# Twelve of fourteen pairs of column tiles by seven block products, and an order by matmul count for every engine

## The chip, the cores and the metric

The kernel runs on one core of one Trainium2 chip. The time is the device time of one execution in microseconds (us); the profile adds one execution recorded by the hardware profiler.

## What is computed

One residual block on 1024 tokens of 1024 channels, all in float32. The input is normalised per token, one projection gives eight parts of 512 columns, two mixers use them, and an output projection, a residual and a last norm follow.

```python
h = rmsnorm(x, norm_gain)                              # [1024, 1024]
q, f_logit, i_in, z_a, u, gate_b, gate_c, z_b = split(h @ w_in)   # 8 x 512 columns
f = lb + (1 - lb) * sigmoid(f_logit)                   # 4 heads of 128
o_a = hgrn2_chunkwise(q, log f, 1 - f, i_in)           # chunks of 64 tokens, state 128x128
o_a = rmsnorm_per_head(o_a) * hgrn_norm_gain * silu(z_a)
y_b = gate_b * causal_conv3(gate_c * u)
o_b = rmsnorm_per_64_channels(y_b) * conv_norm_gain * silu(z_b)
x = x + concat(o_a, o_b) @ w_out
out = rmsnorm(x) * final_norm_gain
```

## The kernel before, in words

**Products.** Every operand of a large product is split into two float32r parts, high and low (`split_part`, L96 to 98: ScalarE copies the high part, VectorE subtracts it for the low one). A product of one 128x128 block with 512 columns is then three matmuls (high x high, high x low, low x high), here called *main* products: `pe.mm` at L44 issues each of them. x lies transposed in `XH` and `XL`, channels on partitions, without its norm's factor; that factor (`rst` per token, `R` spread over partitions) is multiplied in when a result is read from PSUM.

**Stages.** First unit v (L156 to 173): the values `i_in` with tokens on partitions, contraction outermost, all eight PSUM banks at once, 192 main products, while x and the weights come in. Then come column tiles of 128 channels on partitions, each two halves of 512 tokens, `project` (L226): 24 main products a half. For each of four heads f and q (`head`, L239), then for each of four conv tiles u, c, b, z (`conv`, L339). Then z_a with tokens on partitions (192) and the output projection (384, the last tile in two halves of 256 columns). That is 24 column tiles of 48; in all 1896 main products of 512 columns and 48 of 256.

**The recurrence.** For each head, `forget` values give cumulated decays `e` (scan, L257) and their reciprocals (L260), and from them `kh` and `qh`. Eight steps follow, one per pair of chunks: `scores` (L287: a product and a transpose on PE, a copy on ACT, a masked copy into `sc` on DVE, L296) and `combine` (L298: up to three products, L306 to L309; the new state on DVE, L317). These small products are put between the main products of the next tiles: `Stream.later` (L49) files a step with the number of main products after which it is due, and `mm` (L43) issues one due step after each main product; `STEP` (13) main products lie between two combines.

**Norm sums of the conv group.** `norm` (L361): the squares of y, split, are multiplied by a 128x128 matrix `bones` of 1/64, which sums 64 partitions and spreads the sum at once: two products of 512 columns for each half tile (L364, L365), then square root, reciprocal and scale (L366 to L369).

**What sets the order.** PE and SP (the queue that issues the DMAs) run in program order; VectorE, ScalarE and GpSimd are ordered by the scheduler, with a priority for the states (L314). PSUM: `psa`, four banks for column tiles, `psb`, four for small steps. Weights go through three staging buffers and six buffers each of high and low parts.

Of the kernel before, what the change touches and what calls it, by code (L numbers as in the profile page):

```python
# [16 lines left out]
P = 128  # L17
# [8 lines left out]
WB = 6       # weight units on chip  # L26
STEP = 13    # main matmuls between the steps of a head's recurrence
NLAG = 44    # main matmuls between a conv tile and its norm's sums
NWARM = 8
AHEAD = 200  # priority of the recurrence's state over other elementwise work  # L30
TLAG = 22    # main matmuls between a gate's product and its transposes

# columns of the packed per-partition constants
C_NG, C_HLB, C_CW, C_CG = 0, 8, 16, 28
NCOL = 32

class Stream:
# [14 lines left out]

    def flush(self):
        while self.heap:
            heapq.heappop(self.heap)[2]()

@with_exitstack
def hybrid_block(ctx: ExitStack, tc: tile.TileContext, xT, x, wtok, wcol, wout, cols, hgain, fgain, out):
# [16 lines left out]

# [8 lines left out]
    ga = const.tile([P, W], F32, name="ga")  # L84

# [1 line left out]
    units = [("v", kp, wtok[0, kp]) for kp in range(4)]  # L87
    for h in range(NH):
        units += [("f", h, wcol[2 * h + 1]), ("q", h, wcol[2 * h])]
    for j in range(4):  # L90
        units += [(c, j, wcol[8 + 4 * j + i]) for i, c in enumerate("ucbz")]
    units += [("za", kp, wtok[1, kp]) for kp in range(4)]
    units += [(f"o{n}", kp, wout[n, kp]) for n in range(2) for kp in (2, 3, 0, 1)]
    split, issued = {}, [0]

    def split_part(hi, lo, raw):  # L96
        A.copy(hi, raw)
        V.tensor_tensor(lo, raw, hi.bitcast(F32), op=ALU.subtract)  # L98
# [12 lines left out]
    def need(c, i):
        pos = next(p_ for p_, u in enumerate(units) if u[0] == c and u[1] == i)
        fetch(pos + WB)
        return split[c, i]

# [1 line left out]
    pv = [(psa if t < 4 else psb).tile([P, W], F32, tag="ps", name=f"pv{t}") for t in range(NT)]  # L117

    def split_x(k, raw, t0, t1):
        g = col[:, C_NG + k:C_NG + k + 1]  # L120
        rv = raw.rearrange("p (t c) -> p t c", c=P)[:, t0:t1]
        A.activation(XH[:, t0:t1, k, :], rv, AF.Copy, scale=g)
        V.scalar_tensor_tensor(XL[:, t0:t1, k, :], rv, g, XH[:, t0:t1, k, :].bitcast(F32), op0=ALU.mult,
                               op1=ALU.subtract)

    rstart = const.tile([P, W], F32, name="rstart")
    V.memset(rstart[:, :P], 0.0)
    V.memset(rstart[:, P:], 0.0)
    for _ in range(NWARM):  # warms TensorE up while the first loads run
        T.matmul(pv[NT - 1][:, :P], rstart[:, :P], rstart[:, :P], start=True, stop=True)  # L130
# [8 lines left out]
    for t in range(0, NT, 2):  # L139
        nc.sync.dma_start(raw[:, t * P:(t + 2) * P], xT[0, :, t * P:(t + 2) * P])  # L140
        if t == 0:
            nc.sync.dma_start(col, cols)
# [191 lines left out]
    for h in range(NH):  # L334
        head(h)
# [232 lines left out]
```

## Time and profile before

| quantity | value |
|---|---|
| median of 3 runs | 502.87 us (502.83 to 503.73) |
| span of the profiled execution, first to last instruction | 500.7 us |
| what lies around the span, by the median | 2.2 us |
| busy: PE, DVE, ACT, POOL | 491.8, 257.6, 172.7, 157.4 us |
| granted TensorE clock, mean over the span | 0.997 of full speed |
| moved by DMA | 38.93 MB |

The busy time of an engine is what the profile counts inside its instructions; a share of it says nothing yet of a stage, so the views by stretch and the timelines come after it. No time of the profiled execution as a run is listed beside its span; the median of the runs is taken for it. The page's chain of work that ended last holds only the last steps on VectorE and is not used here.

### The profile page before, as it was taken

The numbers are of one execution on the slowest core, as the hardware profiler recorded it, in microseconds if no ns is written. First come the engines' busy times: TensorE is split into PE (matmuls) and PEld (weight loads), VectorE is DVE, ScalarE is ACT, GpSimd is POOL, SyncE is SP. The second block draws the span as 40 slices with busy tenths as digits, with TensorE's granted clock in tenths as the row PEclk, the third lists the DMA queues.
The fourth block names the chain that finished last, engine by engine and source line by source line (L and its number), as shares of the span: only waits on it lengthen the run. The fifth ranks groups of instructions, "written<-read, shape, count | busy, mean of one in ns | idle before, by whom it ended". The sixth has DMA issues, their size and how long they took to land. (4 is left out here: it accounts for less than half of the span.)

```text
span 500.7 us, 5886 instructions
## 1 busy us (share of the span) xinstructions
PE 491.8 (98%) x2288; PEld 402.9 (80%) x2288; DVE 257.6 (51%) x363; ACT 172.7 (34%) x301; POOL 157.4 (31%) x143
## 2 busy tenths in 40 slices
PE   9999999999999999999999999999999999999995
PEld 7778887888888888888888888888888888888884
DVE  4342688948668335285647266552933461132323
ACT  5557722233223223170243127122722341123322
POOL 1000044524315003353658975233432122211000
PEclk9999999999999999999999999999999999999998
DMA  7778621110011110202111111112030171001342
GB/s 218 245 255 258 220 87 43 42 43 13 31 43 43 43 43 8 65 13 85 43 43 42 43 42 42 47 47 76 8 119 0 42 232 42 2 0 63 126 159 93
DMA packets 12699, 38.93 MB, mean 78 GB/s; under 512 B 1536, under 2 KB 2048, under 8 KB 12672
## 3 DMA queue, kind: packets, MB, share of 16 engines
q1 hardware_dynamic: 12672, 38.56, 23.2%
q8 instruction: 18, 0.29, 0.3%
q14 instruction: 9, 0.07, 0.0%
HBM read 34.36 MB, written 4.19 MB: 77 GB/s over the span
## 5 line engine op out<-in xcount | busy, mean ns | idle before, releaser
L44 PE MATMUL po<-wh_o,XL 128*128 128x512 f32 (+1 forms) x136 | 52.0, 382 | 0.0
L44 PE MATMUL po<-wl_o,XH 128*128 128x512 f32 (+1 forms) x136 | 52.0, 382 | 0.0
L44 PE MATMUL po<-wh_o,XH 128*128 128x512 f32 (+1 forms) x136 | 51.9, 382 | 0.0
L253 POOL TENSOR_SCALAR k<-f 128x512 f32<-128x512 f32 x8 | 5.0, 621 | 88.2 <-DVE f L251 88.2
L44 PEld LDWEIGHTS po<-wl_o,XH 128*128 128x128 f32 x136 | 25.5, 188 | 5.5
L44 PEld LDWEIGHTS po<-wh_o,XH 128*128 128x128 f32 x136 | 25.5, 188 | 5.4
L44 PEld LDWEIGHTS po<-wh_o,XL 128*128 128x128 f32 x136 | 25.5, 188 | 5.4
L368 DVE RECIPROCAL rs<-rs 128x512 f32<-128x512 f32 x8 | 26.8, 3353 | 3.7 <-ACT rs L367 3.5
L260 DVE RECIPROCAL ei<-e 128x128 f32<-128x128 f32 x32 | 27.1, 909 | 0.3
L44 PE MATMUL pp_f<-XH,wl_f 128*128 128x512 f32 x64 | 26.3, 411 | 0.0
L44 PE MATMUL pv<-wl_v,XH 128*128 128x512 f32 x64 | 25.6, 400 | 0.6 <-DVE wl_v L98 0.5
L44 PE MATMUL pp_q<-XH,wh_q 128*128 128x512 f32 x64 | 26.0, 407 | 0.0
L44 PE MATMUL pp_f<-XL,wh_f 128*128 128x512 f32 x64 | 26.0, 406 | 0.0
L44 PE MATMUL pp_q<-XH,wl_q 128*128 128x512 f32 x64 | 25.8, 403 | 0.0
L44 PE MATMUL pp_q<-XL,wh_q 128*128 128x512 f32 x64 | 25.8, 403 | 0.0
L44 PE MATMUL pp_f<-XH,wh_f 128*128 128x512 f32 x64 | 25.8, 403 | 0.0
L44 PE MATMUL pza<-wl_za,XH 128*128 128x512 f32 x64 | 25.7, 402 | 0.0
L354 POOL TENSOR_TENSOR cu<-us,R 128x512 f32<-128x512 f32 x8 | 11.3, 1418 | 45.9 <-DVE us L353 45.7
L44 PE MATMUL pv<-wh_v,XH 128*128 128x512 f32 x64 | 25.7, 401 | 0.0
L44 PE MATMUL pp_u<-XH,wl_u 128*128 128x512 f32 x64 | 25.6, 400 | 0.0
L44 PE MATMUL pp_c<-XH,wh_c 128*128 128x512 f32 x64 | 25.5, 399 | 0.0
L44 PE MATMUL pp_u<-XL,wh_u 128*128 128x512 f32 x64 | 25.5, 399 | 0.0
(181 smaller groups left out, 1261.1 us busy)
## 6 DMA issues: line engine op xcount, KB each, us to landing
xr<-x SPq DMA_DIRECT2D x8, 512.0 KB, 4.4
raw_o<-wout SPq DMA_DIRECT2D x8, 512.0 KB, 3.2
xo<-x SPq DMA_DIRECT2D x16, 256.0 KB, 3.4
rawx<-xT SPq DMA_DIRECT2D x7, 512.0 KB, 4.1
out<-y SPq DMA_DIRECT2D x7, 512.0 KB, 2.8
raw_f<-wcol SPq DMA_DIRECT2D x4, 512.0 KB, 3.7
raw_q<-wcol SPq DMA_DIRECT2D x4, 512.0 KB, 5.1
raw_u<-wcol SPq DMA_DIRECT2D x4, 512.0 KB, 3.2
```

The lines of the kernel that those rows point to most:

```text
L44: self.T.matmul(*args, **kw)
L253: G.tensor_scalar(kk, f, -1.0, 1.0, op0=ALU.mult, op1=ALU.add)
L260: V.reciprocal(ei[:, c0:c0 + W // 4], e[:, c0:c0 + W // 4])
L354: G.tensor_tensor(cu[:, 2 + o0:2 + o0 + W], us[hf], rs, op=ALU.mult)
L368: V.reciprocal(rs2, rs2)
```

## The change

**Pairs.** The 24 column tiles of f, q, u, c, b, z and the four of z_a (now also with channels on partitions) are taken in 14 pairs: u with c, f with q, b with z for each of h = 0 to 3, and two pairs of z_a. A pair is a 2x2 block product: the weight blocks B11, B12, B21, B22 (512 channels x 128 columns each) by the blocks A11, A12, A21, A22 of x (512 tokens x 512 channels). The first `NPLAIN` = 2 pairs take eight block products (P1 to P8), the other twelve take seven (M1 to M7), on the differences S1 to S4 of x blocks and T1 to T4 of weight blocks. A block product is 12 main products.

**Where the differences are made.** S1 to S4 are built in place over x by VectorE (`x_sum`) and split under the plain pairs, by the table `work` (key: block of 12 main products since the start of v's second half). T1 to T4 go to the two PSUM banks of `pst` (`t_sum`) and are split from there; `prepare` starts that `LEAD` = 5 block products ahead. x now carries its norm's factor, so `R` goes (`normalise`); the first half of v runs on x without it. Partial results that two outputs share are copied out of PSUM by ScalarE (`keep`) and added by VectorE (`add`).

**Order of all engines.** All five orders are written by hand. `Stream.at` files work for any engine at a number of main products, and `due` issues it; small PE steps come at least `SPACE` = 5 main products apart, combines `STEP` = 18 apart. `psa` has four banks, `psb` two.

**Norm sums.** Squares stay float32 and are not split; they are the stationary operand, and a 128x2 `bones` the moving one, four 2-column products for each half tile; a transpose, a store to memory and two loads spread the factor over partitions again. The reciprocal square roots outside the last norm are powers of -0.5 on GpSimd (`rsqrt`).

**Start.** v is done in two halves of 512 tokens; weights and x come in pieces of 128x512.

Three places of the order. On TensorE, at the norm sums of the first conv tile, before (`pp_z` is the PSUM tile of z, `sh` and `sl` the split squares):

```order
L44 MATMUL pp_z0_0_1801<-XH_81,wl_z0_1203 128x512
L44 MATMUL pp_z0_0_1801<-XH_81,wh_z0_1202 128x512
L44 MATMUL pp_z0_0_1801<-XL_82,wh_z0_1202 128x512
L364 MATMUL pss0_0_1822<-sh0_0_1759,bones_412 128x512
L365 MATMUL pss0_0_1822<-sl0_0_1761,bones_412 128x512
L44 MATMUL pp_z0_0_1801<-XH_81,wl_z0_1203 128x512
```

and now (`pb` and `pd` are banks of pair 3, `hB11` and `lT1` parts of its weight operands, `b0_0` the squares):

```order
L60 MATMUL pb_3_1094<-XH_89,hB11_3_965 128x512
L60 MATMUL pb_3_1094<-XL_90,hB11_3_965 128x512
L60 MATMUL pb_3_1094<-XH_89,lB11_3_966 128x512
L600 MATMUL pss0_0_1129<-bones_125,b0_0_983 128x2 x4
L60 MATMUL pd_3_1137<-XH_89,hT1_3_991 128x512
L60 MATMUL pd_3_1137<-XL_90,hT1_3_991 128x512
L60 MATMUL pd_3_1137<-XH_89,lT1_3_992 128x512
```

The two products of 512 columns became four of 2 columns (x4), and they stand between two block products of a later pair.

On VectorE, at the decays of head 0, before (`f` and `e` are its gate and decays, the scan stands as SCALAR_TENSOR_TENSOR at L257, `wl_` are low parts of weights, `qh` the query times decay):

```order
L251 TENSOR_SCALAR f0_1_568<-fl0_1_565,oml_435,lb_433 128x512
L282 TENSOR_TENSOR qh0_0_621<-pp_q0_0_596,er0_0_534 128x512
L254 COPY rstart_97<-f0_1_568 128x8
L255 MEMSET f0_1_568 128x8
L257 SCALAR_TENSOR_TENSOR e0_1_574<-f0_1_568,rstart_97 128x512
L260 RECIPROCAL ei0_1_576<-e0_1_574 128x128 x4
L264 COPY gt0_479<-e0_1_574 128x8
L98 TENSOR_TENSOR wl_q3_653<-raw_q3_651,wh_q3_652 128x1024
L296 COPY_PREDICATED sc0_414<-mask_405,psc0_0_660 128x128
L277 TENSOR_TENSOR gg0_588<-gt0_479 128x7
L296 COPY_PREDICATED sc1_415<-mask_405,psc0_1_672 128x128
```

and now (`z0` and `b0` are the sums of pair 2, `lT`, `lB` low parts of pair 3, `mb` the conv result):

```order
L463 TENSOR_TENSOR qh0_0_797<-qh0_0_797,e0_0_946 128x512
L314 TENSOR_TENSOR lT2_3_1041<-T2_3_1034,hT2_3_1040 128x512
L430 SCALAR_TENSOR_TENSOR e0_1_1070<-kh0_1_758,zeros_97 128x64 x3
L314 TENSOR_TENSOR lB22_3_1067<-B22_3_937,hB22_3_1066 128x512
L430 SCALAR_TENSOR_TENSOR e0_1_1070<-kh0_1_758,zeros_97 128x64 x5
L397 TENSOR_TENSOR z0_1_1089<-pb_2_897,m5_2_956 128x512
L397 TENSOR_TENSOR b0_1_1092<-pb_2_897,m4_2_1061 128x512
L305 TENSOR_TENSOR T4_3_1095<-B21_3_863,T2_3_1034 128x512
L446 RECIPROCAL ei0_1_1098<-e0_1_1070 128x128
L635 TENSOR_TENSOR mb_93<-mb_93,b0_1_1092 128x512
L446 RECIPROCAL ei0_1_1098<-e0_1_1070 128x128
L314 TENSOR_TENSOR lT4_3_1103<-T4_3_1095,hT4_3_1102 128x512
L479 COPY_PREDICATED sc0_129<-mask_122,psc0_0_1111 128x128
```

The one scan of 512 columns became eight of 64, the reciprocals stand apart, and between them and ahead of the first mask (`sc0`) stand the differences, low parts and sums of the pairs.

On SP, the loads at the start, before:

```order
L138 DMA raw_v0_109<-wtok 128x512
L140 DMA rawx0_108<-xT 128x256
L142 DMA col_87<-cols 128x32
L140 DMA rawx0_108<-xT 128x256 x3
L143 DMA raw_v0_109<-wtok 128x512
L159 DMA rawx1_156<-xT 128x1024
L153 DMA xr0_160<-x 128x1024
L159 DMA rawx2_187<-xT 128x1024
L106 DMA raw_v1_189<-wtok 128x1024
L153 DMA xr1_197<-x 128x1024
```

and now:

```order
L164 DMA wv0_135<-wv 128x512
L176 DMA x0_0_139<-xT 128x512
L178 DMA col_94<-cols 128x36
L164 DMA wv1_156<-wv 128x512
L176 DMA x0_1_160<-xT 128x512
L164 DMA wv2_176<-wv 128x512
L176 DMA x0_2_180<-xT 128x512
L188 DMA vo_92<-x 128x1024
L164 DMA wv3_198<-wv 128x512
L176 DMA x0_3_202<-xT 128x512
L188 DMA vo_92<-x 128x1024
```

Halves of x and of the weights alternate in 256 KB pieces, where whole rows of x (512 KB) and pairs of weight rows were loaded before.

The core of the diff:

```diff
+STEP = 18
+SPACE = 5
+LEAD = 5
...
+OPERAND = {"M1": (A11, "B11"), "M2": (A12, "B21"), "M3": (S4, "B22"), "M4": (A22, "T4"), "M5": (S1, "T1"),
+           "M6": (S2, "T2"), "M7": (S3, "T3")}
+ORDER = ["M1", "M5", "M2", "M6", "M3", "M4", "M7"]
...
+PLAIN = ["P5", "P6", "P7", "P8", "P1", "P2", "P3", "P4"]
+OPERAND.update({"P1": (A11, "B11"), "P2": (A12, "B21"), "P3": (A11, "B12"), "P4": (A12, "B22"), "P5": (S3, "B11"),
+                "P6": (S4, "B21"), "P7": (S3, "B12"), "P8": (S4, "B22")})
...
-        if self.heap and self.heap[0][0] <= self.n:
...
+        self.due()
+        if self.heap and self.heap[0][0] <= self.n and self.n >= self.last + SPACE:
+            self.last = self.n
             heapq.heappop(self.heap)[2]()
+            self.due()
...
+    def due(self):
+        while self.work and self.work[0][0] <= self.n:
+            heapq.heappop(self.work)[2]()
...
+    psa = ctx.enter_context(tc.tile_pool(name="psa", bufs=1, space=PSUM))
+    psb = ctx.enter_context(tc.tile_pool(name="psb", bufs=2, space=PSUM))
+    pst = ctx.enter_context(tc.tile_pool(name="pst", bufs=2, space=PSUM))
...
+    def rsqrt(ap):
+        G.tensor_tensor(ap, ap, mhalf[:, :ap.shape[1]], op=ALU.pow)
...
+    SUMS = {S3: ((0, 0), (0, 0), (1, 0), ALU.subtract), S1: ((1, 0), (1, 0), (1, 4), ALU.add),
+            S2: ((1, 4), (1, 4), (0, 0), ALU.subtract), S4: ((0, 4), (0, 4), (1, 4), ALU.subtract)}
+    def x_sum(which, k, eng):
+        (h0, k0), (h1, k1), (h2, k2), op = SUMS[which]
+        eng.tensor_tensor(x_at(h0, k + k0), x_at(h1, k + k1), x_at(h2, k + k2), op=op)
...
+    bones = const.tile([P, 2], F32, name="bones")
+    G.memset(bones, 0.0)
+    G.memset(bones[0:64, 0:1], 1.0 / 64)
+    G.memset(bones[64:128, 1:2], 1.0 / 64)
...
+    for k in range(NK):
+        load_wv(k)
+        load_x(0, k)
+        if 2 <= k < 6:
+            row_sum(k - 2)
+        if k == 6:
+            stats(0)
+        if k == NK - 1:
+            load_x(1, V_ORDER[1][0])
+            load_x(1, V_ORDER[1][1])
+            half_row_sum(0)
+            half_row_sum(1)
...
+    def t_sum(n, name):
+        b = raws[n]
+        x, y = {"T1": ("B12", "B11"), "T2": ("B22", "T1"), "T3": ("B22", "B12"), "T4": ("B21", "T2")}[name]
+        sums[n, name] = pst.tile([P, W], F32, tag="t", name=f"{name}_{n}")
+        V.tensor_tensor(sums[n, name], b[x], b[y] if y in b else sums[n, y], op=ALU.subtract)
...
+    def split_w(g):
+        n, step = products[g]
+        name = OPERAND[step][1]
+        src = raws[n][name] if name in raws[n] else sums[n, name]
+        hi = hip.tile([P, W], F32R, tag="hi", name=f"h{name}_{n}")
+        lo = lop.tile([P, W], F32R, tag="lo", name=f"l{name}_{n}")
+        A.copy(hi, src)
+        pe.at(4, lambda: V.tensor_tensor(lo, src, f32(hi), op=ALU.subtract))
+        ops[n, name] = hi, lo
...
+    def prepare(g):
...
+        if name[0] == "T" and (n, name) not in sums:
+            if name == "T4" and (n, "T2") not in sums:
+                t_sum(n, "T2")
+            t_sum(n, name)
...
+        pe.at(3, lambda: split_w(g))
...
+        prepare(g + LEAD)
+        product(ps, OPERAND[step][0], ops.pop((n, OPERAND[step][1])), first, resumed=not first)
+        if step in ("M1", "M4", "M5", "M6"):
+            keep({"M1": "m1", "M4": "m4", "M5": "m5", "M6": "u2"}[step], n, ps)
+        elif step == "M2":
+            c11(ps, kept.pop((n, "m1")))
+        elif step == "M3":
+            c12(ps, kept.pop((n, "u2")))
+        else:
+            c22(ps, kept.pop((n, "m5")))
+            c21(ps, kept.pop((n, "m4")))
+    def add(out_, ps, t):
...
+                for i in range(8):
+                    pe.at(i, lambda i=i: scan(i * CH))
...
+                pe.at(9, inverse)
+                for i in range(4):
+                    pe.at(9 + 5 * i, lambda c0=i * P: V.reciprocal(eis[0][:, c0:c0 + P], e[:, c0:c0 + P]))
+                pe.at(27, lambda: G.tensor_tensor(kh, kh, eis[0], op=ALU.mult),
+                      lambda: G.tensor_tensor(ev[:, :, 0, :], ev[:, :, 0, :],
+                                              eis[1][:, :, 0, CH - 1:CH].to_broadcast([P, 4, CH]), op=ALU.mult),
...
+            pe.at(2, lambda: A.copy(kts[pr], psc[:, 1]),
+                  lambda: V.copy_predicated(scbuf[(h * NT + pr) % NS], mask.bitcast(I32), psc[:, 0]))
...
-        def norm(hf, sh, sl):
-            pss = psb.tile([P, W], F32, tag="ps", name=f"pss{j}_{hf}")
-            T.matmul(pss, bones, sh, start=True, stop=False)
-            T.matmul(pss, bones, sl, start=False, stop=True)
...
+        def norm(hf, sq):
+            nm = f"{j}_{hf}"
+            pss = psb.tile([P, 2, 4], F32, tag="ps", name=f"pss{nm}")
+            for t in range(4):
+                T.matmul(pss[:, :, t], sq[:, t * P:(t + 1) * P], bones, start=True, stop=True)
+            r2 = sm.tile([P, 2, 4], F32, tag="r2", name=f"r2{nm}")
+            pe.at(3, lambda: A.activation(r2, pss, AF.Identity, bias=epsc, scale=1.0))
+            pe.at(10, lambda: rsqrt(r2.rearrange("p g t -> p (g t)")))
...
+            def to_rows():
+                prr = psb.tile([2 * 4, P], F32, tag="ps", name=f"prr{nm}")
...
+                rr = sm.tile([2 * 4, P], F32, tag="rr", name=f"rr{nm}", bufs=1)
...
+                pe.at(9, lambda: store(rr))
...
+            def store(rr):
+                rows = dram.tile([2 * 4, P], F32, tag="rows", name=f"rows{nm}")
+                nc.sync.dma_start(rows, rr)
+                pe.at(22, lambda: load(rows))
...
+                for g in range(2):
+                    nc.sync.dma_start(rs2[g * 64:(g + 1) * 64, :],
+                                      rows[g * 4:(g + 1) * 4].rearrange("t p -> (t p)").partition_broadcast(64))
+                pe.at(28, lambda: scale(rs2))
...
+        0: O(0, 0, 1) + N(0, 0) + [L(6)] + O(0, 2) + N(0, 1) + O(0, 3) + H(2, 3) + N(0, 2),
+        1: [L(7)] + N(0, 3, 4) + H(4, 5) + N(0, 5) + B(A11, 0),
+        2: [L(0), lambda: fetch(0, *first)] + H(6, 7) + N(0, 6, 7) + B(A11, 1),
+        3: [L(1)] + B(A11, 2, 3) + [lambda: stats(1)] + B(A12, 0),
+        4: [L(2)] + SW(0) + B(A12, 1, 2),
+        5: [L(3)] + SW(1) + B(A12, 3),
+        6: N(1, 0, 4) + SW(2),
+        7: N(1, 1, 5) + SW(3),
+        8: O(1, 0, 1) + N(1, 2, 6) + [lambda: fetch(1, *first)] + O(1, 2, 3),
+        9: N(1, 3, 7),
+        10: X(S3, 0, 1),
+        11: X(S3, 2, 3),
+        12: X(S1, 0, 1) + B(A22, 0),
...
+        16: XS(S1, 3) + X(S2, 0),
+        17: X(S2, 1, 2) + [lambda: fetch(2, "B11", "B12", "B22", "B21")],
+        18: X(S2, 3) + XS(S2, 0),
+        19: XS(S2, 1, 2),
+        20: XS(S3, 0, 1) + XS(S2, 3) + X(S4, 0),
+        21: XS(S3, 2, 3) + X(S4, 1),
+        22: XS(S4, 0) + X(S4, 2, 3),
+        23: XS(S4, 1),
+        24: XS(S4, 2),
+        25: XS(S4, 3),
```

## Rows read from the trace of the kernel before

**Rows 1.** The page, part 1: engine, busy us (share of the span) xinstructions.

```profile
PE 491.8 (98%) x2288; PEld 402.9 (80%) x2288; DVE 257.6 (51%) x363; ACT 172.7 (34%) x301; POOL 157.4 (31%) x143
```

**Rows 2.** Busy times by stretch: us and (xinstructions) per engine, PEclk, DMA share, GB/s.

```profile
75.00:100.00 25.00, 24.23 (x130) 20.32 (x128) 22.30 (x40) 6.79 (x19) 11.96 (x11) 1.00 0.13 43
...
200.00:250.00 50.00, 50.00 (x217) 40.32 (x216) 29.38 (x28) 14.68 (x16) 24.81 (x22) 1.00 0.16 53
...
490.00:495.00 5.00, 4.58 (x39) 4.38 (x37) 2.44 (x8) 1.91 (x6) 0.00 (x0) 1.00 0.26 105
495.00:501.00 6.00, 0.00 (x0) 0.00 (x0) 1.30 (x5) 1.31 (x4) 0.00 (x0) 0.70 0.23 89
```

**Rows 3.** Timeline of PE, 450 to 456 us: start us, us, what; 26 steps apart.

```profile
449.76 0.40 PE L44 MATMUL po<-wl_o,XH 128*128 128x512 f32 x1
...
455.83 0.40 PE L44 MATMUL po<-wh_o,XH 128*128 128x512 f32 x1
```

**Rows 4.** Groups of PE by form: busy us, mean ns of one, idle before.

```profile
L364 PE MATMUL pss<-sh,bones 128*128 128x512 f32 x8 | 3.1, 391 | 0.0
L365 PE MATMUL pss<-sl,bones 128*128 128x512 f32 x8 | 3.1, 390 | 0.0
```

**Rows 5.** Timeline of all engines, 150 to 156 us: a combine and a score step.

```profile
152.14 0.38 PE L306 MATMUL po<-vo,kt 128*128 128x128 f32 x2
...
152.36 0.39 PE L308 MATMUL po<-st,qh 128*128 128x128 f32 x2
...
152.72 0.48 PE L44 MATMUL pp_q<-XH,wh_q 128*128 128x512 f32 x1
...
153.29 0.48 PE L44 MATMUL pp_q<-XL,wh_q 128*128 128x512 f32 x1
```

**Rows 6.** Timeline of the start, 0 to 14 us: first issue, first split, first product.

```profile
0.80 0.38 SPq L138 DMA_DIRECT2D raw_v<-wtok  x1
...
3.43 0.62 ACT L97 CAST wh_v<-raw_v 128x512 fp32r<-128x512 f32 x1 [1.35 <-DMA raw_v<-wtok]
...
4.91 0.79 PE L44 MATMUL pv<-wh_v,XH 128*128 128x512 f32 x1
```

**Rows 7.** Busy times by stretch, two answers: the loads (last two columns).

```profile
25.00:50.00 25.00, 24.97 (x107) 19.80 (x107) 9.02 (x8) 16.29 (x24) 0.00 (x0) 1.00 0.78 256
30.00:32.00 2.00, 2.00 (x10) 1.62 (x9) 1.15 (x1) 0.82 (x1) 0.00 (x0) 1.00 0.96 336
```

**Rows 8.** Groups of ACT and DVE by form: busy us, mean ns of one, idle before.

```profile
L260 DVE RECIPROCAL ei<-e 128x128 f32<-128x128 f32 x32 | 27.1, 909 | 0.3
...
L257 DVE TENSOR_TENSOR_SCAN e<-f,rstart 128x512 f32<-128x512 f32 x8 | 9.8, 1225 | 0.3
...
L296 DVE COPY_PREDICATED sc<-mask,psc 128x128 f32<-128x128 int32 x32 | 9.5, 297 | 10.7 <-ACT kt L295 10.7
...
L317 DVE SCALAR_TENSOR_TENSOR st<-po,gg,dec 128x128 f32<-128x128 f32 x24 | 8.3, 346 | 17.1 <-PE po L309 17.1
...
L452 DVE SCALAR_TENSOR_TENSOR sga<-pza,rst,sga 128x512 f32<-128x512 f32 x8 | 6.0, 750 | 3.4 <-ACT sga L451 3.4
...
L295 ACT COPY kt<-psc 128x128 f32<-128x128 f32 x32 | 8.6, 268 | 28.8 <-PE psc L293 28.8
...
L353 DVE TENSOR_TENSOR us<-pp_c,us 128x512 f32<-128x512 f32 x8 | 5.5, 691 | 17.2 <-PE pp_c L44 17.2
...
L98 DVE TENSOR_TENSOR wl_v<-raw_v,wh_v 128x512 fp32r<-128x512 f32 x2 | 1.4, 693 | 0.8 <-ACT wh_v L97 0.8
...
L97 ACT CAST wh_v<-raw_v 128x512 fp32r<-128x512 f32 x2 | 1.2, 619 | 2.5 <-DMA raw_v<-wtok 2.5
...
L255 DVE MEMSET f<- 128x8 f32 x8 | 0.5, 65 | 2.6 <-POOL k L253 2.5
```

**Rows 9.** Single lines: duration ns min/median/max, first and last start us, forms.

```profile
L98 DVE TENSOR_TENSOR wl_z<-raw_z,wh_z x4: 1226/2246/2292, 136.8 to 288.5; 128x1024 fp32r<-128x1024 f32 x4
L353 DVE TENSOR_TENSOR us<-pp_c,us x8: 682/692/693, 188.8 to 333.4; 128x512 f32<-128x512 f32 x8
L411 POOL TENSOR_TENSOR vo<-vo,ga x8: 1288/1296/2278, 276.2 to 287.2; 128x512 f32<-128x512 f32 x8
```

**Rows 10.** DMA issues: KB each, median us to landing.

```profile
out<-y SPq DMA_DIRECT2D x2, 256.0 KB, 2.1
```

**Rows 11.** Timeline of all engines, 284 to 292 us: a low part beside POOL.

```profile
288.43 1.30 POOL L394 TENSOR_TENSOR mb<-y,z 128x512 f32<-128x512 f32 x1
288.53 2.28 DVE L98 TENSOR_TENSOR wl_z<-raw_z,wh_z 128x1024 fp32r<-128x1024 f32 x1 [0.16 <-ACT wh_z L97]
```

More of the change, by code (lines that the diff above doesn't have):

```diff
@@ L126, in hybrid_block @@
[L126 to L130, printed above, removed]
-    raw = stage.tile([P, S], F32, tag="st", name="rawx0")
-    w0 = stage.tile([P, 2 * W], F32, tag="st", name="raw_v0")
-    hi = wpool.tile([P, 2 * W], F32R, tag="wh", name="wh_v0")
-    lo = wpool.tile([P, 2 * W], F32R, tag="wl", name="wl_v0")
-    split["v", 0] = hi, lo
@@ L176, in hybrid_block @@
-    ident = const.tile([P, P], F32, name="ident")
-    make_identity(nc, ident)
+    epsc = const.tile([P, 1], F32, name="epsc")
+    ones = const.tile([P, 1], F32, name="ones")
+    zeros = const.tile([P, 1], F32, name="zeros")
+    ident = const.tile([P, P], F32, name="ident")
+    pa = [bank_a(t, f"pv{t}") for t in range(4)]
+    V.memset(zeros, 0.0)
+    V.memset(epsc, EPS)
+    V.memset(ones, 1.0)
+    mhalf = const.tile([P, NT], F32, name="mhalf")
+    V.memset(mhalf, -0.5)
+    for _ in range(NWARM):
+        T.matmul(pa[3][:, :P], zeros.to_broadcast([P, P]), zeros.to_broadcast([P, P]), start=True, stop=True)
@@ new lines, in split_sum, with v_mms @@
+    def split_sum(which, k):
+        h0, k0 = SUMS[which][0]
+        split(XH[:, which, k, :], XL[:, which, k, :], x_at(h0, k + k0))
+    def v_mms(hf, tiles, k):
+        xh, xl = v_parts(hf, k)
+        wh, wl = wvs[k]
+        for t, p_ in enumerate(tiles):
+            c = slice(t * P, (t + 1) * P)
+            pe.mm(p_, xh[:, c], wh, start=(k == V_ORDER[hf][0]), stop=False)
+            pe.mm(p_, xh[:, c], wl, start=False, stop=False)
+            pe.mm(p_, xl[:, c], wh, start=False, stop=(k == V_ORDER[hf][-1]))
@@ new lines, in prepare @@
+    def prepare(g):
+        if g >= len(products):
+            return
+        n, step = products[g]
+        name = OPERAND[step][1]
+        if (n, name) in prepared:
+            return
+        prepared.add((n, name))
+        if name[0] == "T" and (n, name) not in sums:
[3 more added lines that the diff above has]
+        pe.at(3, lambda: split_w(g))
+        if n + 1 < npair and step in ("M6", "M7"):
+            some = {"M6": ("B11", "B12", "B21"), "M7": ("B22",)}[step]
+            pe.at(4, lambda: fetch(n + 1, *[b for b in some if b not in raws.get(n + 1, {})]))
@@ new lines, in product, with bank_b @@
+    def product(ps, a, w, first, last=True, resumed=False):
+        wh_, wl_ = w
+        more = {} if not resumed else {"skip_group_check": True}
+        for k in range(4):
+            c = slice(k * P, (k + 1) * P)
+            pe.mm(ps, wh_[:, c], XH[:, a, k, :], start=(first and k == 0), stop=False, **more)
+            pe.mm(ps, wh_[:, c], XL[:, a, k, :], start=False, stop=False, **more)
+            pe.mm(ps, wl_[:, c], XH[:, a, k, :], start=False, stop=(last and k == 3), **more)
+    def bank_b(name):
+        return psb.tile([P, W], F32, tag="ps", name=name)
@@ new lines, in hybrid_block @@
+    tiles = [bank_b("pv4"), bank_b("pv5"), bank_a(0, "pv6"), bank_a(1, "pv7")]
+    rs1 = t512("rs1", "keep")
+    pe.later(62, lambda: spread(1))
+    pe.at(66, lambda: A.copy(rs1, prs[1]))
+    first = ("B11", "B21", "B12", "B22")
+    L = lambda k: lambda: load_x(1, k)
+    N = lambda hf, *ks: [lambda k=k: normalise(hf, k) for k in ks]
+    B = lambda b, *ks: [lambda k=k: split_a(b, k) for k in ks]
+    X = lambda s, *ks: [lambda k=k: x_sum(s, k, V) for k in ks]
+    XS = lambda s, *ks: [lambda k=k: split_sum(s, k) for k in ks]
```

741 lines of the change are left out of this document (426 added, 315 removed).

## Prediction

> **What bounds the kernel now.** I read first the busy times of the engines: TensorE (PE) works 491.8 of 500.7 us, VectorE (DVE) 257.6, ScalarE (ACT) 172.7, GpSimd (POOL) 157.4 [rows 1]. Then the busy times by stretch: PE is full from 200 to 250 us, idles 0.8 us in the densest stretch of the recurrences (75 to 100 us, where DVE is busy 22.3 of 25 us), and only the last 6 us hold none of its work; the granted clock is 1.00 (the 2.4 GHz level) until PE stops, and 0.70 as a mean over those 6 us [rows 2]. So the time is the length of PE's queue plus a start and a tail that no other engine shortens. The rate comes from the timeline: 26 steps of the 512-column product from 449.76 to 455.83 us, 0.2335 us each [rows 3]. The profiled span is 500.7 us and the median of the runs 502.87, so 2.2 us lie around the span; I make the sum on the span and add them back.
>
> **Products removed.** A pair of column tiles takes 2 x 2 x 8 x 3 = 96 main products before, 7 x 4 x 3 = 84 in seven-product form. The first two of the 14 pairs keep eight; twelve pairs drop 12 each: 144 x 0.2335 = 33.6 us off PE's path. Each of them has its own place in a full queue, so none was hidden.
>
> **Norm sums of the conv group.** 16 products of 512 columns go (8 of L364, 8 of L365 [rows 4]): 16 x 0.2335 = 3.7 us. In come 32 fp32 products with 2 moving columns and 8 transposes of 8 columns. No row has a 2-column product. The nearest is the fp32 128x128 product of the recurrence: L306 starts at 152.14, L308 at 152.36, 0.22 us apart, and the weight load is the same 128 columns. Below: half of that, 0.11 (32 x 0.11 = 3.5); above: a whole interruption by a score step, 152.72 to 153.29 less one product, 0.34 (10.9) [rows 3, 5]. I take 0.22, the row with the same operand, 7.0 us, and 8 x 0.11 = 0.9 for the transposes. The recurrence's own products (0.58 from L306 to the next main product, and 0.34, per step) and the 32 + 8 other transposes stay as many.
>
> Sum without new stalls: 500.7 - 33.6 - 3.7 + 7.0 + 0.9 = 471.3 span, 473.5 in time. It keeps what PE idled before (about 3 us in all). Start and tail are the same code in kind: first product at 4.91 us [rows 6], last tile in two halves.
>
> **Loads at the start.** SP issues 256 KB pieces in a new order. Up to the last weight and x block of the first half of v it is 8 x 0.5 + 4 x 0.5 MiB = 6.3 MB, and PE asks for it at 4.91 + 84 x 0.2335 = 24.5 us. The transfers ran at 256 GB/s over 25 to 50 us, with 78% of the DMA engines' time, and at 336 in the fullest 2 us [rows 7]. At 256 that is 24.6 us after the first issue at 0.80; with the way from landing to a split operand (0.62 ACT + 0.69 DVE [rows 8]) the stall is about 2.5 us, at 336 none. The tightest block of the second half (k=1, behind 10.5 MiB = 11.0 MB: 43 us at 256) is wanted at 41.3 us: 0 to 4.8 us in all, not added to the 2.5. The queue is fed deeper than before (small pieces, eight in flight by its waits), so I take 2.
>
> **VectorE's load.** This is what the change moves most. One head's three pairs are 252 main products on PE: 58.8 us, plus 8 x (0.34 + 0.58) of recurrence and about 2 of norm sums: 68 us. DVE gets in the same time: 12 weight differences, 21 low parts, 12 sums of two partial products, and 6 multiplications (51 tensor-tensor at 0.69: 35.3), 6 of the fused kind at 0.75 (4.5), 16 scans of 64 (one of 512 took 1.225, so 0.15 by length, with the 0.06 of the smallest memset 0.21: 3.4), 8 reciprocals at 0.909 (7.3), 8 masks and 7 states (4.8), 1 of small ones: 56 us, 83% [rows 8]. ACT gets 45 operations of 512 columns at 0.62 and 39 small ones at 0.27 (38 us), POOL 8 of 512 at 1.29 [rows 9] and 4 of half that (13, with the powers some 14). So on average PE stays the longest queue, and a head costs nothing. Worse is the way there. In the second half of v (96 products, 22.4 us) DVE is given 18 fused operations at 0.75, 12 others at 0.69 and nine small ones: 23.1 us. From P7 of pair 1 to the end of pair 2 (156 products, 36.4 us) it is given 41 at 0.69, 4 at 0.75, 16 scans and 4 reciprocals: 38.5 us. A queue that is 2 us behind there meets head 0: the first combine waits for `sc`, whose mask (0.30) stands behind eight scans, two reciprocals and seven tensor-tensor operations issued in the 25 products (5.8 us) ahead of it: 8.6 us by the same rows. The weight parts have five products of lead (60 x 0.2335 = 14 us) and stay covered; the mask has 20 products (4.7 us). Below nothing, above the whole lag of 8 us; I take 2.5, since what is late catches up while PE waits, once, and later heads start from an empty queue.
>
> **Two banks for the small steps.** `psb` has two buffers, not four, for psc, po, pss, prr and pt. Each is freed by DVE or ACT; two steps lie 9 products (2.1 us) apart, so a reuse has some 4.2 us, and with a norm sum between them less. Next to it stands the old kernel's stretch with DVE at 89%, which cost PE 0.8 us [rows 2]. 0 to 4 us over four heads; I take 1.
>
> **Edits I cost at nothing.** The x differences S1 to S4 and their splits run under the plain pairs; the last S4 block is issued 45 products (10 us) before its use. Differences written to PSUM: nearest row L353, 0.69. The power on POOL for each rsqrt: nearest rows are of whole tiles; one as long as a 512-wide product (1.3) at rst's second half would still end about when PE asks for the transposes: 0 to 1 us. The rs2 round trip through memory: two transfers at about 2.1 us [rows 10], against 22 and 28 products (5.1 and 6.5 us) left for them. Fewer table loads and shorter reciprocals help engines that do not bound.
>
> Together 473.5 + 2 + 2.5 + 1 = **479.0 us**.
>
> **Rivals.**
> *No new stall* (chance 0.25). The lags were each enough, loads run above 300 GB/s, and the written order also removes some of the 3 us PE idled: 470.5 to 474. For it: the average loads above. Against: the two dense stretches.
>
> *VectorE partly the bound* (0.2). Operations that read two operands in SBUF do not share with POOL: the low part of a 1,024-wide weight took 1.23 at best and 2.29 at most, and the one from 288.53 us ran 2.28 beside POOL operations, while L353, with a PSUM operand, never took over 0.693; POOL's multiply took 1.29 to 2.28 [rows 9, 11]. If half of POOL's 14 us per head is added to DVE's 56, and DVE does no better than the 89% of its fullest stretch [rows 2], a head takes (56 + 7) / 0.89 = 71 against 68: 3 x 4 = 12 us, about 490.
>
> *Slower* (0.05). The same mechanism in full: all of POOL's time blocks DVE, (56 + 14) / 0.89 = 79 a head, 11 us more than PE's queue, 44 over four heads: 473.5 + 44 = 518. It passes 502.9 when a head needs over 75 us, that is when 11 of POOL's 14 us are added. Against: about half of DVE's time (differences in PSUM, sums from banks, masks from banks) has a PSUM operand, which the rows show undisturbed. The Trainium skill, "SBUF — State Buffer", section "Who interferes with whom", says that a VectorE instruction with two SBUF inputs and a GpSimd one that reads SBUF take a shared port for a whole instruction, and the later one blocks fully. By that rule alone, with every POOL operation meeting such a VectorE one, this rival would hold; by the rows only part of them meet. The trace agrees with the rule itself: 2.29 is 1.23 and most of a POOL operation.
>
> *The change doesn't do what it says*: the order of PE holds 144 + 16 products fewer, so nothing is left of this rival but the stalls above. A result near no change (0.02) needs 29 us of stalls, a mixture of the two last.
>
> **How the numbers follow.** Forecast with small stalls, 475 to 485: 0.48; no new stall 0.25; partly bound by VectorE 0.2; slower 0.05; no change 0.02. The range, 470.5 to 491, takes the first two, and the third up to its price; the bounds of the norm sums (-3.5, +3.9) and of the stalls (0 to 4.8, 8 and 4) lie in it, except all at their worst. A measurement here can tell some 0.2%, 1 us, from no change: faster 0.93, within it 0.02, slower 0.05.
>
> **What would show it.** Right: PE some 460 us busy in a span near 477; 0.2335 us per product unchanged; DVE near 83% over the heads; PE's idle time in few places, at the start (waiting for x or wv) and about the first masks of head 0. Wrong: PE idle spread over all four heads with DVE above 85% (the second rival), a granted clock below 1.00 in the middle, or pss groups over 0.34 us per product.

## The result

The changed kernel takes 489.5 us (488.5 to 491.3, four runs) against 503.3: a ratio of 0.971, with a 95% interval of 0.966 to 0.975. That is 13.8 us less where 23.9 were forecast; the range of 470.5 to 491 holds it. Executions far slower than the others of their kernel (among them one of early_sums, its profiled one, and one of norm_later) are left out of the times below. The page of the changed kernel, its span, its busy times and its clock by slices, answers to [rows 1]:

```profile
span 486.8 us, 6267 instructions
...
PE 466.8 (96%) x2200; PEld 383.1 (79%) x2200; DVE 328.1 (67%) x593; ACT 232.2 (48%) x553; POOL 99.1 (20%) x92
...
PEclk9999999999799999999998999998999999999999
```

PE works 25.0 us less than before and idles 20.0 us of the span where it idled 8.9. VectorE (328.1 us) and ScalarE (232.2) have gained what the block differences cost, and POOL has lost 58 us. The clock row is new: it is not at 9 in three places, where before only the end was. The waits of PE, by what it waited for (us in total, times, longest):

```profile
PE psc L475 <- DVE sc L479: 5.0, 1, 5.0
...
PE pss L600 <- DVE sc L479: 3.6, 3, 1.4
...
PE po L60 <- ACT woh L753: 1.9, 1, 1.9
...
PE pv L60 <- ACT XH L179: 1.0, 1, 1.0
...
PE pt L679 <- DVE lT L314: 0.6, 1, 0.6
...
PE po L60 <- DVE wol L754: 0.2, 1, 0.2
```

With 1.0 at the warm-up products that is 13.3 us; before, four such rows made 2.7, of them 1.1 at the warm-up and 0.5 for `pv`. The others here are new. `sc` is the masked score that VectorE copies out of a bank of `psb`. The other loss is in three stretches, behind three of the waits for `sc` (columns as in [rows 2]; the first row is of the loads):

```profile
5.00:25.00 20.00, 19.35 (x83) 15.60 (x84) 12.31 (x22) 16.31 (x31) 1.40 (x1) 1.00 1.04 383
125.60:130.60 5.00, 5.00 (x13) 4.07 (x14) 3.72 (x6) 1.92 (x5) 3.51 (x5) 0.51 0.00 0
263.80:267.20 3.40, 3.40 (x11) 2.82 (x11) 2.42 (x6) 0.58 (x2) 2.57 (x2) 0.52 0.00 0
335.30:338.70 3.40, 3.40 (x12) 2.85 (x11) 2.96 (x7) 1.06 (x5) 2.41 (x2) 0.51 0.03 8
```

In the last three stretches PE is busy all the time at a granted clock of 0.51 or 0.52 (the 1.2 GHz level nearly throughout). They are 5.0, 3.4 and 3.4 us long. Six steps of the 512-column product, from 127.22 to 129.78 us (below), took 0.427 us each there, where [rows 3] have 0.2335; by this estimate 45% of the 11.8 us, 5.3 us, are lost. The first row answers to [rows 7]: the loads ran at 383 GB/s as a mean over 20 us.

Against the sum of the prediction, 471.3 us of span: the norm sums cost 0.89 us a group where 0.88 was taken (0.1 for eight), waits add 13.3 - 2.7 = 10.6 and the clock 5.3. That makes 487.3, and the span is 486.8. One difference is not in this list: in the output projection a product stepped 0.2285 us (314 steps from 402.37 to 474.12 us) where [rows 3] have 0.2335, 1.9 us over its 384 products. Something else must make up for it, so that the list closes to 0.5 us is in part chance.

**Head 0.** The longest wait, on the timeline of all engines:

```profile
116.37 1.29 POOL L646 TENSOR_TENSOR z<-z,sg 128x512 f32<-128x512 f32 x1 [1.43 <-ACT sg L645]
116.41 2.81 DVE L430 TENSOR_TENSOR_SCAN e<-kh,zeros 128x64 f32<-128x64 f32 x3
...
116.66 0.38 PE L475 MATMUL psc<-qh,kh 128*128 128x128 f32 x2
...
117.74 1.33 POOL L647 TENSOR_TENSOR mb<-mb,z 128x512 f32<-128x512 f32 x1
...
118.39 0.95 PE L600 MATMUL pss<-bones,b 128*128 128x2 f32 x8
...
119.20 0.48 PE L60 MATMUL pd<-XH,hT 128*128 128x512 f32 x1
...
119.72 1.01 DVE L430 TENSOR_TENSOR_SCAN e<-kh,zeros 128x64 f32<-128x64 f32 x5
...
120.21 0.40 PE L60 MATMUL pd<-XL,hT 128*128 128x512 f32 x1
...
125.23 0.28 DVE L479 COPY_PREDICATED sc<-mask,psc 128x128 f32<-128x128 int32 x1
...
125.57 0.79 PE L475 MATMUL psc<-qh,kh 128*128 128x128 f32 x2 [4.96 <-DVE sc L479]
...
127.22 0.63 PE L60 MATMUL pd<-XL,hT 128*128 128x512 f32 x1
...
129.78 0.63 PE L60 MATMUL pa<-XL,hB 128*128 128x512 f32 x1
```

The first score's product stands at 116.66 us (it ends at 117.04) and its mask ends at 125.51. From 120.6 on PE waits for it: the second score (L475 at 125.57, 4.96 us idle) needs a bank of `psb`, one has the first score in it and the other the norm sum of L600. VectorE is in the middle of the scans of the second half when the score ends. Three scans took 2.81 us, beside two POOL multiplications of 1.29 and 1.33, and the next five 1.01. The norm sum's four products take from 118.39 to 119.20, 0.81 us, and the products behind them start another 0.08 us late: from 119.20 to 120.21 are four steps, 1.01 us in place of 0.93. That is 0.89 us a group.

**Heads 1 to 3.** Here the norm sum is the third step: it follows the two scores and waits for the bank of the first. At head 2:

```profile
260.47 0.59 ACT L313 CAST hT<-T 128x512 fp32r<-128x512 f32 x1 [3.09 <-DVE T L305]
...
261.48 0.42 ACT L478 COPY kt<-psc 128x128 f32<-128x128 f32 x2
...
261.77 0.30 DVE L479 COPY_PREDICATED sc<-mask,psc 128x128 f32<-128x128 int32 x1 [0.80 <-ACT kt L478]
```

The mask ends 5.7 us behind its score (256.36 to 262.07), but it does not stand behind VectorE's work: VectorE idles 0.80 us ahead of it and waits for ScalarE's copy `kt` out of the same bank. That copy stands in ScalarE's queue behind a cast that had waited 3.09 us for a difference `T` of VectorE. One operation of VectorE ahead of that difference, a low part at 257.42 us, took 1.76 us beside a POOL multiplication of 1.28. Heads 1 and 3 show the same waits of 3.09 and 0.80 us. No run has the copy ahead of the cast, so what that would give is open.

**Start of the output projection**, SP's queue first:

```profile
380.84 9.07 SPq L810 DMA_DIRECT2D xo<-x  x3
...
390.90 1.60 SPq L749 DMA_DIRECT2D wo<-wout  x3
...
396.60 0.62 ACT L753 CAST woh<-wo 128x512 fp32r<-128x512 f32 x1 [10.15 <-DMA wo<-wout]
...
397.27 0.50 PE L60 MATMUL po<-woh,XH 128*128 128x512 f32 x1 [1.90 <-ACT woh L753]
```

SP stands 9.07 us at the residual loads, whose third needs a buffer; three weight loads issue behind them at 390.90, and the first of these lands for the 1.90 us wait at 397.27.

### The profile page after: what moved, and what is told of

Read it like the earlier page. It is cut to its first block, busy times and chain, and to the rows that moved or that the text cites. A ratio compares the mean times of both kernels' runs of the same rounds, so it can differ in the third digit from the quotient of the medians.

```text
span 486.8 us, 6267 instructions
## 1 busy us (share of the span) xinstructions
PE 466.8 (96%) x2200; PEld 383.1 (79%) x2200; DVE 328.1 (67%) x593; ACT 232.2 (48%) x553; POOL 99.1 (20%) x92
## 4 chain that ended last, share of the span: by engine, by line
PE 62%; DVE 23%; ACT 9%; issue 3%; DMA 2%; SPq 0%; POOL 0%; DVEq 0%; ACTq 0%; POOLq 0%
PE po L60 16%; PE pb L60 10%; PE pv L60 9%; PE p L60 7%; PE pd L60 6%; DVE ei L446 4%; PE pa L60 4%; DVE e L430 3%; DVE T L305 3%; DVE lB L314 3%; PE pe L60 3%; DVE lT L314 1%; ACT hT L313 1%; PE pss L600 1%; PE po L492 1%
## 5 line engine op out<-in xcount | busy, mean ns | idle before, releaser
L313 ACT CAST hT<-T 128x512 fp32r<-128x512 f32 x48 | 28.2, 587 | 94.7 <-DVE T L305 77.1
L314 DVE TENSOR_TENSOR lB<-B,hB 128x512 fp32r<-128x512 f32 x44 | 34.2, 776 | 16.8 <-ACT hB L313 14.2
L314 DVE TENSOR_TENSOR lT<-T,hT 128x512 fp32r<-128x512 f32 x48 | 32.7, 682 | 11.8 <-ACT hT L313 11.6
L60 PE MATMUL pb<-XH,lT 128*128 128x512 f32 x96 | 39.3, 409 | 0.0
L60 PE MATMUL pb<-XH,hT 128*128 128x512 f32 x96 | 38.5, 401 | 0.0
L60 PE MATMUL pb<-XL,hT 128*128 128x512 f32 x96 | 38.5, 401 | 0.0
L60 PE MATMUL po<-XH,XL 128*128 128x512 f32 (+1 forms) x88 | 32.7, 372 | 0.1
L313 ACT CAST hB<-B 128x512 fp32r<-128x512 f32 x44 | 27.2, 623 | 11.6 <-issue 11.6
L60 PE MATMUL po<-XH 128*128 128x512 f32 (+1 forms) x88 | 32.7, 371 | 0.0
L60 PE MATMUL po<-XL,XH 128*128 128x512 f32 (+1 forms) x88 | 32.6, 371 | 0.0
```

Source lines behind the costliest of these rows:

```text
L313: A.copy(hi, src)
L314: pe.at(4, lambda: V.tensor_tensor(lo, src, f32(hi), op=ALU.subtract))
```

## Experiments

All are edits of the changed kernel, and times are compared with its 489.5 us; ratios are to the kernel before. The changed kernel was not run again beside them; the kernel before took 503.3 to 503.7 us in the same sessions, so a difference of 1 us between two versions says little. The theory to test: the first mask of each head comes late, through VectorE, the two banks of `psb` carry that lateness to PE, and POOL's operations make part of it. The rivals: VectorE's load alone is the bound, or the banks alone.

**Half banks (slots4).** `psc`, `po`, `pss` and `prr` go in turn to the four halves of two banks.

```diff
...
-            psc = psb.tile([P, 2, P], F32, tag="ps", name=f"psc{n_}")
+            psc = half_b().rearrange("p (a c) -> p a c", c=P)
...
```

> The two banks of psb are used as four half banks, so that a second score or a norm sum need not wait until the first score's bank is read; nothing else changes. Theory (a late mask on VectorE costs PE time because only two small steps can be open): the waits of 1.36, 1.11 and some 1.1 us at the starts of heads 1 to 3 go, and with them the two half-clock phases behind the last two (1.7 us each); at head 0 the mask, 8.9 us behind its score in the changed kernel, is now waited for by the first combine, 22 products and some 1 us of small steps later, so 2.4 us of the 5.0 stay. About 480 us. Rival (VectorE is simply too full there, whatever the banks): the same waits stand before the combines, 487 to 491 us.

518.7 us, ratio 1.028 (1.021 to 1.036). The expectation failed, by the way the edit works: the norm sum (L608 here), in the other half of the first score's bank, waits for the mask.

```profile
119.24 0.38 PE L483 MATMUL small<-qh,kh 128*128 128x128 f32 x2
...
127.80 0.28 DVE L487 COPY_PREDICATED sc<-mask,small 128x128 f32<-128x128 int32 x1
...
128.13 1.01 PE L608 MATMUL small<-bones,b 128*128 128x2 f32 x4 [7.00 <-DVE sc L487]
```

Halves of a bank were not independent places here; with successive steps in one bank there was in effect one open step, and the wait grew to 7.00 us. So it shows the price of one open step in place of two (29 us), not the gain of one more. The Trainium skill, "PSUM — Partial Sum Buffer", section "PSUM bank collisions raise a hardware error", asks to guard PSUM by bank and partition quadrant, not by address; this run behaves so, though it can't tell whether bank or tile set the waits.

**Heads started later (late).**

```diff
-            pe.at(62, tasks[n][1])
+            pe.at(78, tasks[n][1])
...
-            pe.at(90, tasks[1][1])
+            pe.at(114, tasks[1][1])
```

> The small steps of head 0 start 24 main products later and those of heads 1 to 3 16 later; banks and everything else as in the changed kernel. Theory (VectorE's lag of 8.0 us at head 0's first mask and some 4 to 5 us at the others is passing): with 5.6 us more at head 0 and 3.7 at the others VectorE is within 2 banks' reach again, the waits of 5.0, 1.36, 1.11 and 1.1 us shrink to under 2 in all and no half-clock phase follows: about 479 to 482 us. Rival (the lag does not pass, since VectorE is the bound around each head's start): same waits at the new place, 487 to 491 us.

494.5 us, ratio 0.980 (0.974 to 0.986). Head 3 then ends so late that its first 512 tokens go into their gate ahead of their normalisation. PE's waits:

```profile
PE pt L679 <- POOL vo L540: 8.1, 1, 8.1
...
PE prr L607 <- POOL r L198: 5.2, 1, 5.2
...
PE po L489 <- DVE sc L479: 1.9, 1, 1.9
```

Of the waits for a mask one of 1.9 us is left. But VectorE is still late, and its lateness reaches PE by another way: the power for the norm sum (`r`, L198) stands in POOL's queue behind a multiplication that needs VectorE's reciprocals, and the transpose `prr` waits 5.2 us for it. At the end a gate's transpose waits 8.1 us for head 3's scale. Neither theory forecast this.

**POOL's multiplications later (pool_later).**

```diff
-                pe.at(10, lambda: G.tensor_tensor(z, z, sg, op=ALU.mult))
-                pe.at(16, lambda: G.tensor_tensor(y, y, z, op=ALU.mult))
+                pe.at(50, lambda: G.tensor_tensor(z, z, sg, op=ALU.mult))
+                pe.at(56, lambda: G.tensor_tensor(y, y, z, op=ALU.mult))
```

> GpSimd's two multiplications of the conv gate (z by its sigmoid, y by z) come 40 main products later, so that they no longer stand beside the scans ahead of head 0's first mask. Theory (GpSimd blocks VectorE there: three scans of 64 took 2.81 us where five took 1.01): the three scans take 0.6 us, the mask comes some 2.2 us earlier, the wait of 5.0 becomes about 2.8, and with a shorter half-clock phase the time is about 486 us. Rival (the long scans have another cause, or the lag is VectorE's own work): three scans still near 2.8 us, 489 to 490 us.

487.6 us, ratio 0.967 (0.962 to 0.973).

```profile
118.09 0.65 DVE L430 TENSOR_TENSOR_SCAN e<-kh,zeros 128x64 f32<-128x64 f32 x3
...
118.36 0.38 PE L475 MATMUL psc<-qh,kh 128*128 128x128 f32 x2
...
125.13 0.29 DVE L479 COPY_PREDICATED sc<-mask,psc 128x128 f32<-128x128 int32 x1
...
125.47 0.77 PE L475 MATMUL psc<-qh,kh 128*128 128x128 f32 x2 [3.17 <-DVE sc L479]
```

The same three scans take 0.65 us, and the wait is 3.17 us in place of 4.96.

**The same multiplications on VectorE (gate_dve).**

```diff
-                pe.at(10, lambda: G.tensor_tensor(z, z, sg, op=ALU.mult))
-                pe.at(16, lambda: G.tensor_tensor(y, y, z, op=ALU.mult))
+                pe.at(10, lambda: V.tensor_tensor(z, z, sg, op=ALU.mult))
+                pe.at(16, lambda: V.tensor_tensor(y, y, z, op=ALU.mult))
```

> GpSimd's two multiplications of the conv gate are given to VectorE at the same places of the order. Theory (beside them VectorE stood still for 2.2 us): VectorE gets three of them, 2.1 us, ahead of head 0's first mask and gets back the 2.2 us, so that the wait there stays near 5 us and the time within 1.5 us of 489.5, though VectorE has 16 operations more, 11 us. Rival (nothing is blocked, VectorE's own work is all): the mask comes 2.1 us later, the wait is 7 us, and the other heads wait longer too: over 492 us.

488.9 us, ratio 0.970 (0.966 to 0.974).

```profile
117.98 0.68 DVE L646 TENSOR_TENSOR z<-z,sg 128x512 f32<-128x512 f32 x1
...
118.69 0.69 DVE L647 TENSOR_TENSOR mb<-mb,z 128x512 f32<-128x512 f32 x1
...
119.30 0.65 DVE L430 TENSOR_TENSOR_SCAN e<-kh,zeros 128x64 f32<-128x64 f32 x3
...
126.30 0.80 PE L475 MATMUL psc<-qh,kh 128*128 128x128 f32 x2 [4.11 <-DVE sc L479]
```

Two of the multiplications stand ahead of the scans (0.68 and 0.69 us), the scans take 0.65, and PE waits 4.11 us. Sixteen operations more on VectorE cost nothing. So at head 0 POOL's two operations took more from VectorE (2.16 us at the scans) than they spared it (1.37). Elsewhere VectorE has idle time, and this run does not tell which of the sixteen fell into it.

**Norm sums later (norm_later).**

```diff
-                pe.later(60 if j == 0 else 44, lambda: norm(hf, b))
+                pe.later(84 if j == 0 else 68, lambda: norm(hf, b))
```

> The norm sums of the conv group come 24 main products later, so that none of them takes one of the two psb banks between the first two scores of a head; VectorE's work keeps its order but for what follows the norm sums. Theory (with two banks the third small step waits for the first mask): at head 0 the second score finds a free bank and the wait moves to the first combine, 22 products and some 0.3 us behind the first score: 3.4 us instead of 5.0; at heads 1 to 3 some 0.5 us each instead of 1.1 to 1.36. About 486 us. Rival (only VectorE's lag decides, the banks do not): the same waits in sum, 489 to 490 us.

486.4 us, ratio 0.964 (0.961 to 0.968).

```profile
118.67 0.38 PE L475 MATMUL psc<-qh,kh 128*128 128x128 f32 x2
...
120.87 0.39 PE L475 MATMUL psc<-qh,kh 128*128 128x128 f32 x2
...
127.24 0.28 DVE L479 COPY_PREDICATED sc<-mask,psc 128x128 f32<-128x128 int32 x1
...
127.57 0.49 PE L489 MATMUL po<-vo,kt 128*128 128x128 f32 x2 [2.94 <-DVE sc L479]
```

The second score runs 2.2 us behind the first with no wait, and the first combine (L489) waits 2.94 us for `sc`. The mask's lag is the same 8.5 us (119.05 to 127.52), so at head 0 the banks decide, beside the lag. PE's waits of 1 us and more, the warm-up and `pv` apart:

```profile
PE po L489 <- DVE sc L479: 4.5, 3, 2.9
PE po L60 <- ACT woh L753: 3.3, 1, 3.3
PE psc L475 <- DVE lT L314: 1.8, 1, 1.8
...
PE psc L475 <- ACT po L508: 1.1, 3, 0.4
```

The waits for a mask fell from 8.6 to 4.5 us, but a score of head 3 now waits 1.8, three scores 1.1 for another bank, and the output weights cost 3.3 in place of 1.9. All waits together are 13.3 us, as in the changed kernel. The gain therefore does not lie in the sum of PE's waits; what did go is two of the three half-clock stretches (one is left, from 395.8 to 399.2 us).

**x differences earlier (early_sums).** The blocks of the table `work` move up, for instance:

```diff
...
-        20: XS(S3, 0, 1) + XS(S2, 3) + X(S4, 0),
-        21: XS(S3, 2, 3) + X(S4, 1),
-        22: XS(S4, 0) + X(S4, 2, 3),
...
+        18: XS(S2, 3) + X(S4, 0),
+        19: X(S4, 1, 2, 3),
+        20: XS(S3, 0, 1),
+        21: XS(S3, 2, 3) + XS(S4, 0),
...
```

> The x differences S1, S2 and S4 and the splits of S1, S2 and S4 are filed 6 to 36 main products earlier, into the end of v and pair 0, where VectorE runs level with TensorE; the amount of work is the same. Theory (the lag of 3.9 us that VectorE has from 348 products on comes from these sums and is carried to head 0's first mask): the mask comes about 2 us earlier, the wait of 5.0 becomes about 3, and the time 487 us. Rival (the lag at the mask is made by the work of pair 3 alone): 489 to 490 us.

486.6 us, ratio 0.965 (0.962 to 0.969), as the theory has it. That the mask came earlier is not read from this run itself; the combination below bears on it.

**Weight loads first (loads_first).**

```diff
-    residual(0)
-    residual(1)
...
     for i in range(5, NK):
         pe.at(2 + 6 * (i - 5), load_out(0, OUT_ORDER[i]))
+    residual(0)
+    residual(1)
```

(The loads of `gf` stay ahead of the loop.)

> The last three weight loads of the output projection are issued ahead of the residual loads on SP. Theory (SP waits 9.5 us for a buffer of the residual and the three weight loads queue behind it; PE then waits 2.1 us for the sixth weight block): the wait of 2.1 us at the start of the output projection goes, about 487.4 us. Rival (the loads land no earlier, or the residual's loads then make VectorE late for the first output tile): 489 to 490 us.

486.2 us, ratio 0.964 (0.957 to 0.971): 3.4 us where 2.1 were expected. PE no longer waits for a part of these weights; the rest is within what runs of this kernel differ by (488.5 to 491.3).

**Together (combo): pool_later, loads_first, early_sums.**

> Three changes together: GpSimd's gate multiplications 40 products later, the last weight loads of the output projection ahead of the residual loads, and the earlier x differences. Theory (the three waits have separate causes and add): 1.9 + 2.1 + 2 us off the changed kernel, 483 to 484 us. Rival (they share one limit, VectorE's total load): 486 us or more.

480.9 us, ratio 0.954 (0.951 to 0.956): 8.6 us less than the changed kernel, where the three edits by themselves took 1.9, 3.4 and 2.9, and 2 us better than expected. The waits that are left behind a mask:

```profile
PE pss L600 <- DVE sc L479: 3.5, 3, 1.3
...
PE psc L475 <- DVE sc L479: 1.0, 1, 1.0
```

Head 0's wait (`psc`) is 1.0 us, so the earlier differences took 2.1 us off the 3.17; the norm sums of heads 1 to 3 (`pss`) wait as before, and behind each of them the clock is at the 1.2 GHz level for 3.4 us (from 187.0, 258.7 and 330.4 us).

**Together with later norm sums (combo_norm24, combo_norm12):** the edit of norm_later, by 24 and by 12.

> The three changes of combo and the norm sums 24 main products later as well. Theory (what is left in combo at heads 1 to 3, waits of 1.3 us each of a norm sum for the first mask and three half-clock phases of 1.7 us, hangs on the two banks): the waits fall to 0.5 to 0.8 us each, moved to the first combine, and some or all of the half-clock phases go; at head 3 a score may wait 1.8 us longer, as in the run with later norm sums alone. 477 to 479 us. Rival (the half-clock phases have another cause): 479.5 to 481 us.

> As the run before, with the norm sums 12 main products later in place of 24: the norm sum still stands behind the second score but asks for its bank 2.8 us later, when the first mask of heads 1 to 3, 1.3 us late, is done. Theory (a wait is the mask's lateness less what lies between): no wait at heads 1 to 3 and no half-clock phase behind one, 476 to 479 us, at head 3 no longer wait of a score. Rival (other small steps take the bank in its place): 480 to 481 us.

476.2 us (ratio 0.945, 0.943 to 0.948) and 475.2 us (0.943, 0.941 to 0.946). The page of the second, and PE from its first product to 460 us:

```profile
span 472.6 us, 6239 instructions
...
PE 462.0 (98%) x2200; PEld 378.5 (80%) x2200; DVE 329.8 (70%) x593; ACT 231.6 (49%) x553; POOL 98.5 (21%) x92
...
PEclk9999999999999999999999999999999999999998
```

```profile
4.90:460.00 455.10, 452.12 (x2135) 369.15 (x2136) 324.40 (x575) 225.74 (x541) 96.65 (x78) 1.00 0.26 86
```

PE idles 3.0 us in 455 us and the clock never leaves 1.00 until PE stops: with the waits the three half-clock stretches went too. The span of 472.6 us is 1.3 us over the prediction's sum without new stalls. This version beats both kernels: 28.2 us less than before, twice the gain of the change.

## Why the prediction was right or wrong

**Products removed and norm sums: right.** A product took 0.2335 us as forecast in the pairs and less, 0.2285, in the output projection; a group of four norm products cost 0.89 us (0.88 taken), their transpose 0.11 as taken (0.03 up to the next product at 134.91 us, 0.08 behind it). The last experiment bears out the sum as a whole, with a span 1.3 us above it.

**Loads at the start: taken 2, came out at some 0.5.** PE waits 1.0 us for x where it waited 0.5 for a weight part before. The transfers ran at 383 GB/s, above the 336 of the fullest stretch read before. (At 256 GB/s the text's own terms, 24.6 + 0.8 + 1.31 - 24.5, make 2.2 us of stall, not 2.5.)

**VectorE's lag: right place and lag, wrong step that waits.** The prediction put the whole lag at 8 us, and the mask ended 8.5 us behind its score (117.04 to 125.51). It let the first combine, 20 products behind the score, be what waits for it, and took 2.5 us. That path is seen by itself in norm_later, where the same lag costs 2.94 us at the first combine. In the changed kernel another step asks first: the second score needs the bank that the late mask still reads, and PE waited 4.96 us. So the 2.5 was near the price of the path that the text had, and the path was the wrong one. Part of the lag was not length of operations but standing still beside POOL, 2.2 us at the scans, which the sum had left to a rival. "Later heads start from an empty queue" held for VectorE, which idles just ahead of the first mask at heads 1 to 3, and the masks were late all the same, through ScalarE's queue, whose load the text had summed and whose order it had not followed.

**Two banks: taken 1, came to 3.6** at heads 1 to 3, with three waits of up to 1.4 us, and to some 2.0 of head 0's 4.96 (4.96 - 2.94). The text named a norm sum between two steps, but took each bank to be freed in time; it did not ask how late the mask that frees the first one is, and which step stands third behind it. It was a norm sum, and moving it by 12 products took nearly all of these waits away (0.2 us is left at each head).

**The granted clock: not in the sum, 5.3 us.** The text spoke of a clock below 1.00 only as a sign of error. A stall has to be costed with the half-clock stretch that may follow it.

**The output weights: not looked for, 2.1 us.** The new order of SP was followed at the start only, not where the residual loads wait for a buffer.

**The power on POOL.** The text let it be as long as a 512-column multiplication, 1.3 us; the eight of the norm sums took 1.64 each. PE did not wait for one in the changed kernel; in late one of 2.08 us stands in the wait of 5.2.

**The rivals.** "VectorE partly the bound" named 490, close to the time, but its mechanism did not hold as told. PE's waits stand at one place in each head, not spread over it. VectorE is busy 23.2 of 25 us from 100 to 125 us, where head 0 starts, but 167 of 225 us (74%) from 125 to 350 us, where the prediction had 83% over the heads. What held is its cause, in places: VectorE does stand still beside POOL. The Trainium skill, "SBUF — State Buffer", section "Who interferes with whom", lets a VectorE instruction with two SBUF inputs and a GpSimd one that reads SBUF use a shared port only one after the other. The trace agrees for the scan, whose two inputs lie in SBUF: three took 2.81 us beside POOL, 0.65 without. The change did what it said; the slower cases did not occur.

The range holds the time because its upper end was taken from this rival's price. As that price came from another mechanism than the one that acted, this part is luck: the forecast itself, 479.0, was 10.5 us short.

## What to carry to other kernels

When the work of the longest queue is cut, follow for each small step the queue ahead of what frees its buffer, through every engine in it, and take off only the way to the first step that asks for that buffer: a late mask and two banks cost 8.6 us of waits here, though over the span no engine but PE was near full. Putting one other step 12 products later took 5.7 us off the combination, the two edits that made the mask earlier 1.9 and 2.9. And read the issuing queue wherever a load waits for a buffer, because everything behind it waits too.

## What the runs showed of the hardware

In the changed kernel the granted clock fell to 0.50 (the 1.2 GHz level) three times: at 123.7 us, 3 us into head 0's wait of 4.96, and 1.5 and 1.9 us after PE had taken up work again behind waits of 1.11 and 1.12 us (263.7 after 262.1, 335.3 after 333.5). It stayed at 1.00 behind a wait of 1.36 us (at 192 us), behind the one of 1.90 (at 397 us) and behind those of 1.01 us and less.

The length of a wait does not tell these cases apart. In pool_later the clock fell behind a wait of 1.31 us (at 191.5 us; 0.50 from 193.9 to 197.1) and not behind one of 1.11 (at 262.9 us). In norm_later it stayed at 1.00 behind 2.94 us (at 127.6 us) and fell behind 3.29 (at 394.7 us). What decides is open, so which waits are followed by such a stretch is a part of the difference between two of these runs that no edit here controls.
